# mv of a second mLSTM head made ahead of the first block, with scaled copies of x^T moved behind it

## The chip, the cores and the metric

One core of a Trainium2 chip runs the whole program. The metric is device microseconds for one execution. TensorE is called PE here, its weight loads PEld, VectorE DVE, ScalarE ACT, GpSimd POOL; SyncE (SP) and POOL issue most of the DMAs.

## The reference

One encoder layer on x of 512 positions by 2048 features, all in float32. A normalised x goes through one input projection that feeds an mLSTM branch (4 heads, run forwards and backwards), a differential attention branch (8 heads) and two branch gates; then an output projection, a gated feed-forward part and a last norm follow.

```python
h = _rmsnorm(x, norm1_w[l])
proj = h @ w_in[l]
mq, mk, mv, mo, mg, aq, ak, av, gt = jnp.split(proj, IN_OFFSETS, axis=-1)
q = mq.reshape(B, S, M_HEADS, M_DQK)
v = mv.reshape(B, S, M_HEADS, M_DV)
...
h_fwd = _mlstm_scan(q, k, v, ig[0], lf[0])
...
hm = _rmsnorm(hm, mlstm_norm_w[l].reshape(M_HEADS, M_DV))
hm = hm * jax.nn.sigmoid(mo).reshape(B, S, M_HEADS, M_DV)
```

What the change touches is `v`, the values of the four mLSTM heads: 512 positions by 256 columns each, x (normalised) times a 2048 by 256 slice of `w_in`.

## The kernel before, in words

Each float32 product is made of three float32r matmuls: both operands are split into a rounded part (`hi`, a cast on ACT, L149 or L602) and the rest (`lo`, a subtraction on DVE, L150 or L603), and `mm3` (L145) multiplies hi by hi, hi by lo and lo by hi.

The large projections (the block functions `pre_chunk`, `wo_chunk`, `fi_chunk`, `fo_chunk`) use a scheme of seven products instead of eight (`seven`): per group of 512 contraction rows the left side is needed in seven forms, which are quarters of x^T (`X11`, `X12`, `X22`) and sums of quarters (`S1` to `S4`). The first such block makes the attention values (`av0`). The small projections (`aqk`, `mqk`, `mv`, by `proj_a` and `proj_b`) are plain.

Work is written as chunks, generators that yield after some matmuls. `one()` runs the next step of the first chunk in the list; `advance(ns)` runs steps worth so many nanoseconds between the parts of attention and mLSTM; `upto(name)` runs all up to a chunk's end; `until` runs steps until a condition holds. `behind` is a list of small jobs, and `work()` takes one of them at each step. A scheduler then orders the instructions of each engine; each engine runs its own list in order.

At the start `mv_first` (L725) sets up chunk `mv0`: mv of head 0 with the 16 gate columns, 16 steps of 12 matmuls of 128x272. Its left side is x^T itself, one 128x512 tile (`xraw`) per step. The loop over those 16 tiles (L1324 on) loads each, splits it (two 128x256 `hi` on ACT, L602, two `lo` on DVE, L603), and makes two plain float32 scaled copies on ACT (L1337), of which `xfactors` (L1285) makes the sums `S1` to `S4` (on DVE) and splits them. After each group of four tiles the jobs s1, s2, s34 of that group go to `behind`, and after all four groups the eight jobs that make S4 and S3. Then `av0` begins.

The result of mv0 is copied from PSUM by ACT (L732), written to DRAM by POOL (L735), and fetched back when head 0 of the mLSTM begins. Heads 1 to 3 of mv are chunks of 192 matmuls of 128x256 each (`mv_chunk`, L753), which stand among the chunks `mqk` and run as filler between parts of attention and of the mLSTM; their result is scaled and split straight from PSUM (`mv_split`, L744). `mlstm(h)` (L1195) fetches four tiles of the output gate (`mo`) and two rows of running maxima (`nM`) through POOL, makes the weights (`md`, `mw`), the score matmuls (`ms`), splits them (`mah`, `mal`) and multiplies with v (`mn`). `square` (L1358) loads the 16 natural tiles of x (`xnat`) through POOL one after another and squares them on ACT, for the norm.

Buffers that matter: weights `raw` 6, `hi` 3, `lo` 3; 39 tiles of 128x512 (`t_`); 16 tiles of 128x1024 (`x_`); 8 PSUM banks.

Of the kernel before, what the change touches and what calls it, by code (L numbers as in the profile page):

```python
# [12 lines left out]
F32 = mybir.dt.float32  # L13
# [7 lines left out]
P = 128  # L21
# [10 lines left out]
MH = 4  # L32
# [82 lines left out]
def build(ctx, tc, a, out):  # L115
# [21 lines left out]
    def sm(name, n, tag=None, bufs=None):  # L137
        return small.tile([P, n], F32, tag=tag or name, name=name, bufs=bufs)
# [424 lines left out]
    mv0d = [dpool.tile([P, 512], F32, name=f"mv0_d{i}") for i in range(2)]  # L563

    def rope(p, name, scale, key):
        t = t_(f"{name}_t")
# [155 lines left out]

    def mv_first():  # L725
        def post(view):
            g = sm("g_raw", 64, bufs=1)
            env["g"] = g
            for i in range(2):
                raw = t_(f"mv0_{i}")  # L730
                for t in range(2):
                    A.copy(raw[:, t * 256:(t + 1) * 256], view[2 * i + t][:, :256])  # L732
                    V.tensor_copy(g[:, (2 * i + t) * 16:(2 * i + t + 1) * 16],
                                  view[2 * i + t][:, 256:272])
                G.dma_start(mv0d[i], raw)  # L735

        def lhs(kk, t):
            f_ = xf[kk // 4][f"X{t // 2 + 1}{kk % 2 + 1}"]
            sl = slice(t % 2 * P, t % 2 * P + P)
            return [p_[:, kk % 4 // 2, sl] for p_ in f_]  # L740
        chunk("mv0", [a["w_mv0"][i] for i in range(8)], 2, 272,
              lambda n, it: proj_b(n, it, True, lhs, post, lambda kk: work()))

    def mv_split(h, view):  # L744
        vh = ppool.tile([P, NT, 258], F32R, tag="p", name=f"mvh{h}")
        vl = ppool.tile([P, NT, 258], F32R, tag="p", name=f"mvl{h}")
        V.tensor_copy(vh[:, :, 256:258], ones[:, 0:8].rearrange("p (t c) -> p t c", c=2))
        V.tensor_copy(vl[:, :, 256:258], zero[:, 0:8].rearrange("p (t c) -> p t c", c=2))
        for t in range(NT):
            scaled_split(view[t][:, :256], rstd1[:, t:t + 1], vh[:, t, 0:256], vl[:, t, 0:256])  # L750
        mval[h] = (vh, vl)

    def mv_chunk(h):  # L753
        def lhs(kk, t):
            return [p_[:, t * P:(t + 1) * P] for p_ in xs[kk]]

        def post(view):
            mv_split(h, view)
            while h == MH - 1 and len(has) < AH:
                ha_split()  # L760


        def step(kk):
            if kk % 2 == 0:
                ha_fetch()
            elif kk > 4:
                ha_split()
        chunk(f"mv{h}", [a["w_mv"][(h - 1) * 4 + i] for i in range(4)], 4, 256,
              lambda n, it: proj_b(n, it, False, lhs, post, step if h == MH - 1 else None))
# [499 lines left out]
            hm.append(o)  # L1269


    mv_first()
    n1w = const.tile([P, KD], F32, name="c_n1w")
    nc.sync.dma_start(n1w, a["n1w"])


    xraw, xX = [], []

    def xload(again=False):
        k = len(xraw)  # L1280
# [3 lines left out]

    def xfactors(g):  # L1285

        X, out, nm = xX[g], xf[g], f"x{g}"

        def s1():
            X["S"] = half(f"{nm}_S")  # L1290
            V.tensor_tensor(X["S"], X["X21"], X["X22"], ALU.subtract)
            factor(nm, False, out, "S1", X["S"])

        def s2():
            V.tensor_tensor(X["S"], X["S"], X["X11"], ALU.subtract)
            factor(nm, False, out, "S2", X["S"])

        def s34():
            V.tensor_tensor(X["X21"], X["X11"], X["X21"], ALU.subtract)
            V.tensor_tensor(X["X12"], X["X12"], X["S"], ALU.add)  # L1300
        return ([s1, s2, s34], [lambda: factor(nm, False, out, "S4", X["X12"]),
                                lambda: factor(nm, True, out, "S3", X["X21"])])


# [19 lines left out]
    for k in range(KD):  # L1324
        g, j, s_ = k // 4, k % 2 + 1, k % 4 // 2
        if k % 4 == 0:
            xX.append(fresh(f"x{g}"))
# [156 lines left out]
```

## Time and profile before

| what | us |
|---|---|
| median of 3 runs | 2639.59 (2639.15 to 2642.4) |
| the profiled execution, its own time | 2640.17 |
| its span | 2637.6 |
| TensorE busy | 2592.7 (98%) |
| VectorE busy | 2120.6 (80%) |
| ScalarE busy | 1297.7 (49%) |
| GpSimd busy | 240.0 (9%) |

The span is the time between the first and the last instruction of the profile; the profiled execution took 2.6 us more than its span. Matmuls are pipelined, so that a row's duration is longer than the step from one matmul to the next; the step is read from start times. The same holds, to a smaller extent, for ACT and DVE.

### The profile page before, as it was taken

What the parts mean: (1) busy time and instruction counts of PE and PEld (TensorE: products, weight loads), DVE (VectorE), ACT (ScalarE), POOL (GpSimd) and SP (SyncE); (2) the same over time, 40 slices, a digit from 0 to 9 for tenths busy, and PEclk for the clock granted to TensorE, in tenths of its full rate; (3) what the DMA queues carried; (4) which work ended last, traced back from release to release, by engine and by line L of the source; (5) the groups of instructions that cost most, each with busy time, mean ns of one, the idle gap of its engine ahead of it and who ended that gap; (6) DMA issues with size and microseconds to landing.
All of it is one profiled execution on the core that took longest, in us unless ns stands there. A gap on an engine that the chain in (4) does not pass through costs nothing. (4 is left out here: it accounts for less than half of the span.)

```text
span 2637.6 us, 33224 instructions
## 1 busy us (share of the span) xinstructions
PE 2592.7 (98%) x12184; PEld 2160.2 (82%) x12184; DVE 2120.6 (80%) x2684; ACT 1297.7 (49%) x1824; POOL 240.0 (9%) x440
## 2 busy tenths in 40 slices
PE   8999999999999999999999999999999999999998
PEld 7888888878889998887788888888888878788886
DVE  8877888778875675587898887888888879989985
ACT  8544444545543453344464444444444445556554
POOL 1000000011110123100200000000000001212220
PEclk9999999999999999999999999999999999999999
DMA  7655556744432346446755555555554578777772
GB/s 252 231 189 185 200 192 218 244 125 127 121 115 78 122 141 237 176 153 210 264 184 174 195 178 183 182 196 187 180 197 167 175 279 302 253 274 255 244 247 83
DMA packets 161203, 508.97 MB, mean 193 GB/s; under 512 B 21832, under 2 KB 22120, under 8 KB 161040
## 3 DMA queue, kind: packets, MB, share of 16 engines
q1 hardware_dynamic: 110304, 377.68, 41.5%
q0 software_dynamic: 31536, 95.62, 11.2%
q10 hardware_dynamic: 19200, 33.57, 3.6%
q8 instruction: 95, 1.56, 0.2%
q14 instruction: 68, 0.56, 0.1%
HBM read 445.41 MB, written 50.87 MB: 188 GB/s over the span
## 5 line engine op out<-in xcount | busy, mean ns | idle before, releaser
L145 PE MATMUL aqk_b<-xs,whi_aqk 128*128 128x512 f32 x512 | 161.4, 396 | 0.0
L149 ACT CAST whi_fi_Q<-fi_Q_t 128x1024 fp32r<-128x1024 f32 x88 | 92.5, 1052 | 117.8 <-PE fi_b L145 96.1
L145 PE MATMUL fi_a<-whi_fi_Q,h_X 128*128 128x512 f32 x440 | 147.1, 392 | 0.0
L145 PE MATMUL fi_c<-whi_fi_Q,h_S 128*128 128x512 f32 x440 | 144.6, 390 | 0.0
L145 PE MATMUL fi_b<-whi_fi_Q,h_S 128*128 128x512 f32 x352 | 115.5, 389 | 0.0
L145 PEld LDWEIGHTS aqk_b<-xs,whi_aqk 128*128 128x128 f32 x512 | 94.6, 189 | 18.2
L150 DVE TENSOR_TENSOR wlo_fi_Q<-fi_Q_t,whi_fi_Q 128x1024 fp32r<-128x1024 f32 x88 | 106.3, 1218 | 3.2 <-ACT whi_fi_Q L149 3.1
L362 DVE TENSOR_TENSOR raw_fi_e<-raw_fi_e,raw_fi_f 128x1024 f32<-128x1024 f32 x44 | 53.8, 1224 | 63.8 <-DMA raw_fi_e<-in_w_ffi 63.7
L145 PE MATMUL aqk_b<-xs,wlo_aqk 128*128 128x512 f32 x256 | 100.4, 392 | 0.0
L145 PEld LDWEIGHTS fi_c<-whi_fi_Q,h_S 128*128 128x128 f32 x440 | 82.5, 188 | 17.0
L145 PEld LDWEIGHTS fi_a<-whi_fi_Q,h_X 128*128 128x128 f32 x440 | 82.6, 188 | 16.8
L145 PE MATMUL fi_c<-wlo_fi_Q,h_S 128*128 128x512 f32 x220 | 86.0, 391 | 0.6 <-DVE wlo_fi_Q L150 0.6
L145 PE MATMUL fi_a<-wlo_fi_Q,h_X 128*128 128x512 f32 x220 | 85.7, 389 | 0.7 <-DVE wlo_fi_Q L150 0.7
L990 POOL DMA_DIRECT2D fs_X<-fg_X11d x22 | 11.9, 540 | 795.8 <-DVE wlo_fi_Q L150 737.7
L348 DVE TENSOR_TENSOR raw_fi_b<-raw_fi_b,raw_fi_a 128x1024 f32<-128x1024 f32 x44 | 53.8, 1223 | 35.7 <-DMA raw_fi_b<-in_w_ffi 28.1
L149 ACT CAST whi_fi_Q<-raw_fi_e 128x1024 fp32r<-128x1024 f32 x44 | 46.4, 1055 | 72.6 <-PE fi_b L145 54.3
L149 ACT CAST whi_fi_Q<-raw_fi_b 128x1024 fp32r<-128x1024 f32 x44 | 46.5, 1056 | 72.3 <-PE fi_c L145 52.7
L145 PE MATMUL ba_p<-whi_ba,hahl 128*128 128x512 f32 x256 | 82.0, 390 | 0.0
L145 PE MATMUL bm_p<-whi_bm,hmhl 128*128 128x512 f32 x256 | 80.6, 391 | 0.0
L145 PE MATMUL mqk_b<-xs,whi_mqk 128*128 128x512 f32 x256 | 80.4, 394 | 0.0
L149 ACT CAST whi_fi_Q<-raw_fi_f 128x1024 fp32r<-128x1024 f32 x44 | 46.5, 1056 | 68.3 <-PE fi_c L145 63.7
L145 PEld LDWEIGHTS fi_b<-whi_fi_Q,h_S 128*128 128x128 f32 x352 | 66.1, 188 | 13.7
(830 smaller groups left out, 8425.8 us busy)
## 6 DMA issues: line engine op xcount, KB each, us to landing
raw_fi_a<-in_w_ffi SPq DMA_DIRECT2D x44, 512.0 KB, 4.2
raw_fi_b<-in_w_ffi SPq DMA_DIRECT2D x44, 512.0 KB, 4.2
raw_fi_c<-in_w_ffi SPq DMA_DIRECT2D x44, 512.0 KB, 4.3
raw_fi_d<-in_w_ffi SPq DMA_DIRECT2D x44, 512.0 KB, 4.3
raw_fi_f<-in_w_ffi SPq DMA_DIRECT2D x44, 512.0 KB, 3.9
raw_fi_e<-in_w_ffi SPq DMA_DIRECT2D x44, 512.0 KB, 3.9
raw_aqk<-in_w_aqk SPq DMA_DIRECT2D x32, 512.0 KB, 3.5
raw_fo_a<-in_w_ffo SPq DMA_DIRECT2D x20, 512.0 KB, 4.2
```

The source lines that it names most:

```text
L145: T.matmul(dst, lhs[l], rhs[r], start=first and i == 0, stop=last and i == 2, skip_group_check=skip)
L149: A.copy(hi, src)
L150: V.tensor_tensor(lo, src, hi.bitcast(F32), ALU.subtract)
L348: V.tensor_tensor(raws[r12], raws[r12], raws[r11], ALU.add)
L362: V.tensor_tensor(raws[r12], raws[r12], raws[r22], ALU.add)
L990: G.dma_start(got[n], fgd[g][f_].rearrange("p (k c) -> p k c", k=2))
```

## The change

- A second head of mv, `mv1`, becomes a chunk between `mv0` and the first block. Its left side is the split quarters of x^T that mv0 uses, its weights are four loads of 512 KB, and it has 16 steps at which `work()` takes a job.
- The scaled copies of x^T leave the loop over tiles. They are now two jobs per group in `behind` (eight ACT instructions a group), ahead of s1, s2 and s34 of that group.
- All heads of mv are now kept: copied from PSUM by ACT, written to DRAM by POOL (`mv_keep`), fetched back by POOL (`mv_fetch`) and split from there. Head h+1 is fetched ahead of `mlstm(h)`, after `upto("mv{h+1}")`.

```diff
+    def mv_keep(h, view):
+        for i in range(2):
+            raw = t_(f"mv{h}_{i}")
+            for t in range(2):
+                A.copy(raw[:, t * 256:(t + 1) * 256], view[2 * i + t][:, :256])
+            G.dma_start(mvd[h][i], raw)
...
-        chunk("mv0", [a["w_mv0"][i] for i in range(8)], 2, 272,
-              lambda n, it: proj_b(n, it, True, lhs, post, lambda kk: work()))
+        if h == 0:
+            chunk("mv0", [a["w_mv0"][i] for i in range(8)], 2, 272,
+                  lambda n, it: proj_b(n, it, True, lhs, post, lambda kk: work()))
+        else:
+            chunk(f"mv{h}", [a["w_mv"][(h - 1) * 4 + i] for i in range(4)], 4, 256,
+                  lambda n, it: proj_b(n, it, False, lhs, post, lambda kk: work()))
+    mvraw = {}
+    def mv_fetch(h):
+        mvraw[h] = [t_(f"mv{h}r{i}") for i in range(2)]
+        for i in range(2):
+            G.dma_start(mvraw[h][i], mvd[h][i])
+    def mv_split(h):
+        view = [mvraw[h][t // 2][:, t % 2 * 256:t % 2 * 256 + 256] for t in range(NT)]
...
-            mv_split(h, view)
+            mv_keep(h, view)
...
-    mv_first()
+    for h in range(2):
+        mv_first(h)
...
+        X, out, nm = {}, xf[g], f"x{g}"
+        def scaled(j):
+            for i in (1, 2):
+                X[f"X{i}{j}"] = half(f"{nm}_X{i}{j}")
+            for s_ in range(2):
+                k = 4 * g + 2 * s_ + j - 1
+                for i in (1, 2):
+                    A.activation(X[f"X{i}{j}"][:, s_], xraw[k][:, (i - 1) * 256:i * 256], AF.Copy,
+                                 scale=n1w[:, k:k + 1])
...
-        return ([s1, s2, s34], [lambda: factor(nm, False, out, "S4", X["X12"]),
+        return ([lambda: scaled(1), lambda: scaled(2), s1, s2, s34], [lambda: factor(nm, False, out, "S4", X["X12"]),
...
-        for i in range(2):
-            f_, src = f"X{i + 1}{j}", xraw[k][:, i * 256:i * 256 + 256]
-            A.activation(xX[g][f_][:, s_], src, AF.Copy, scale=n1w[:, k:k + 1])
...
-        if h:
+        if h > 1:
             mv_chunk(h)
...
     for h in range(MH):
-        if h:
-            upto(f"mv{h}")
+        upto(f"mqk{h}")
+        mv_split(h)
         if h == MH - 1:
             hm_split()
+        else:
+            upto(f"mv{h + 1}")
+            mv_fetch(h + 1)
         mlstm(h)
```

How the change moves instructions, at three places. First the queue of SyncE at the start (`raw_mv_50` to `raw_mv_70` are the last weights of mv0, `raw_mv_00` and those after it the weights of mv1, `xraw` tiles of x^T from the seventh on, `raw_av` weights of the first block). Before:

```order
L197 DMA raw_mv_50_278<-in_w_mv 128x544
L197 DMA raw_mv_60_280<-in_w_mv 128x544
L197 DMA raw_mv_70_282<-in_w_mv 128x544
L1283 DMA xraw_314<-in_xT 128x512
L1283 DMA xraw_338<-in_xT 128x512
L1283 DMA xraw_362<-in_xT 128x512
L1283 DMA xraw_390<-in_xT 128x512
L197 DMA raw_av_a_732<-in_w_pre 128x1024
L197 DMA raw_av_b_734<-in_w_pre 128x1024
L1283 DMA xraw_420<-in_xT 128x512
L197 DMA raw_av_c_736<-in_w_pre 128x1024
```

And now:

```order
L197 DMA raw_mv_50_278<-in_w_mv 128x544
L197 DMA raw_mv_60_280<-in_w_mv 128x544
L197 DMA raw_mv_70_282<-in_w_mv 128x544
L197 DMA raw_mv_00_288<-in_w_mv 128x1024
L197 DMA raw_mv_10_294<-in_w_mv 128x1024
L1300 DMA xraw_316<-in_xT 128x512
L197 DMA raw_mv_20_318<-in_w_mv 128x1024
L1300 DMA xraw_340<-in_xT 128x512
L197 DMA raw_mv_30_342<-in_w_mv 128x1024
L1300 DMA xraw_364<-in_xT 128x512
L1300 DMA xraw_386<-in_xT 128x512
```

Two of the four loads of mv1's weights now stand ahead of the seventh tile of x^T (`xraw_316`), one ahead of the eighth and one ahead of the ninth; the block's first weights come after all but three of the tiles.

Second, ACT in the same stretch (L602: the `hi` of a tile of x^T; L1337 before and L1312 now: the scaled copies; `whi_mv`: `hi` of mv0's weights). Before:

```order
L602 ACTIVATE x_X_381<-xraw_266,c_n1w 128x256
L602 ACTIVATE x_X_383<-xraw_266,c_n1w 128x256
L1337 ACTIVATE x_X_377<-xraw_266,c_n1w 128x256
L1337 ACTIVATE x_X_379<-xraw_266,c_n1w 128x256
L602 ACTIVATE x_X_380<-xraw_314,c_n1w 128x256
L602 ACTIVATE x_X_382<-xraw_314,c_n1w 128x256
L1337 ACTIVATE x_X_376<-xraw_314,c_n1w 128x256
L149 CAST x_S2h<-x_S 128x512
L1337 ACTIVATE x_X_378<-xraw_314,c_n1w 128x256
L149 CAST whi_mv_50_449<-raw_mv_50_278 128x544
L602 ACTIVATE x_X_381<-xraw_338,c_n1w 128x256
L602 ACTIVATE x_X_383<-xraw_338,c_n1w 128x256
```

And now:

```order
L602 ACTIVATE x_X_379<-xraw_340,c_n1w 128x256
L602 ACTIVATE x_X_381<-xraw_340,c_n1w 128x256
L1312 ACTIVATE x_X_388<-xraw_242,c_n1w 128x256
L1312 ACTIVATE x_X_389<-xraw_242,c_n1w 128x256
L1312 ACTIVATE x_X_388<-xraw_250,c_n1w 128x256
L1312 ACTIVATE x_X_389<-xraw_250,c_n1w 128x256
L1312 ACTIVATE x_X_416<-xraw_246,c_n1w 128x256
L1312 ACTIVATE x_X_417<-xraw_246,c_n1w 128x256
L1312 ACTIVATE x_X_416<-xraw_254,c_n1w 128x256
L1312 ACTIVATE x_X_417<-xraw_254,c_n1w 128x256
L602 ACTIVATE x_X_485<-xraw_364,c_n1w 128x256
L602 ACTIVATE x_X_487<-xraw_364,c_n1w 128x256
```

The scaled copies stood in pairs behind each tile; now the eight of the first group stand in one piece between the eighth tile and the ninth. On PE, 21 of mv1's 192 matmuls now stand ahead of the last matmul of mv0, spread over its last three steps; the other 171 follow it, and then the block.

Third, POOL where the first head of the mLSTM begins (`mv0r`, `mv1r`: heads of mv fetched back; `ha_d<-hn`: the last head of attention written out; `mo`, `nM`: see above). Before:

```order
L1452 DMA mv0r_7827<-mv_d_124 128x512
L1452 DMA mv0r_7828<-mv_d_125 128x512
L1108 DMA ha_d<-hn_7811 128x512
L1200 DMA mo_0_7885<-mo_d_1888 128x256
L1200 DMA mo_0_7885<-mo_d_1892 128x256
L1200 DMA mo_1_7886<-mo_d_1965 128x256
L1200 DMA mo_1_7886<-mo_d_1969 128x256
L1205 DMA nM_0_7891<-negm_d 128x512
L1205 DMA nM_1_7893<-negm_d 128x512
```

And now:

```order
L730 DMA mv_d_128<-mv_0_7987 128x512
L730 DMA mv_d_129<-mv_1_7991 128x512
L757 DMA mv0r_8037<-mv_d_124 128x512
L757 DMA mv0r_8038<-mv_d_125 128x512
L1124 DMA ha_d<-hn_8021 128x512
L757 DMA mv1r_8077<-mv_d_126 128x512
L757 DMA mv1r_8078<-mv_d_127 128x512
L1216 DMA mo_0_8081<-mo_d_2120 128x256
L1216 DMA mo_0_8081<-mo_d_2124 128x256
L1216 DMA mo_1_8082<-mo_d_2197 128x256
L1216 DMA mo_1_8082<-mo_d_2201 128x256
L1221 DMA nM_0_8087<-negm_d 128x512
```

The two writes of head 2 of mv stand ahead of the fetch of head 0, and the fetch of head 1 stands ahead of `mo` and `nM` of head 0. The same holds for heads 1 and 2, with the fetches of heads 2 and 3.

## Rows read from the trace of the kernel before

**Rows 1.** the page: the span, and busy time, share and instructions of each engine
```profile
span 2637.6 us, 33224 instructions
...
PE 2592.7 (98%) x12184; PEld 2160.2 (82%) x12184; DVE 2120.6 (80%) x2684; ACT 1297.7 (49%) x1824; POOL 240.0 (9%) x440
```

**Rows 2.** busy time in three stretches; columns as in the first line
```profile
core 0: us, PE busy (x) PEld busy (x) DVE busy (x) ACT busy (x) POOL busy (x), PEclk, DMA share, GB/s
...
0.00:100.00 100.00, 87.10 (x424) 74.43 (x425) 84.30 (x132) 74.01 (x151) 15.09 (x35) 0.97 0.73 247
...
20.00:40.00 20.00, 16.47 (x105) 14.94 (x106) 20.00 (x40) 19.99 (x48) 0.00 (x0) 0.92 0.68 235
...
800.00:900.00 100.00, 100.00 (x691) 92.81 (x691) 56.21 (x116) 39.81 (x78) 8.24 (x13) 1.00 0.27 93
```

**Rows 3.** longest wait of TensorE in the whole run: total us, times, longest
```profile
PE mv_p L145 <- ACT whi_mv L149: 6.8, 1, 6.8
```

**Rows 4.** timeline of TensorE, 20 to 64 us: start, us, instruction, [idle before]
```profile
20.29 0.28 PE L145 MATMUL mv_p<-whi_mv,x_X 128*128 128x272 f32 x1
...
35.49 0.39 PE L145 MATMUL mv_p<-whi_mv,x_X 128*128 128x272 f32 x1 [1.82 <-DVE x_X L603]
...
43.65 0.40 PE L145 MATMUL av_a<-whi_av_Q,x_X 128*128 128x512 f32 x1
...
46.87 0.39 PE L145 MATMUL av_c<-wlo_av_Q,x_S1h 128*128 128x512 f32 x1
...
51.63 0.39 PE L145 MATMUL av_b<-whi_av_Q,x_S2l 128*128 128x512 f32 x1
...
63.91 0.39 PE L145 MATMUL av_a<-whi_av_Q,x_X 128*128 128x512 f32 x1
```

**Rows 5.** timeline of TensorE inside one later head of mv
```profile
941.08 0.28 PE L145 MATMUL mv_p<-wlo_mv,xs 128*128 128x256 f32 x1
...
944.68 0.28 PE L145 MATMUL mv_p<-wlo_mv,xs 128*128 128x256 f32 x1
```

**Rows 6.** busy time in two stretches of 2 us, columns as in rows 2
```profile
22.00:24.00 2.00, 1.54 (x13) 1.32 (x11) 2.00 (x6) 2.00 (x5) 0.00 (x0) 1.00 1.02 391
...
38.00:40.00 2.00, 2.00 (x11) 2.00 (x11) 2.00 (x6) 1.99 (x5) 0.00 (x0) 0.50 0.01 2
```

**Rows 7.** timelines of VectorE, 41 to 45 us, and of ScalarE, 23 to 25 us
```profile
41.73 0.88 DVE L603 SCALAR_TENSOR_TENSOR x_X<-xraw,c_n1w,x_X 128x256 fp32r<-128x256 f32 x2
...
42.60 0.69 DVE L1291 TENSOR_TENSOR x_S<-x_X,x_X 128x512 f32<-128x512 f32 x1
...
43.20 1.22 DVE L150 TENSOR_TENSOR wlo_av_Q<-raw_av_a,whi_av_Q 128x1024 fp32r<-128x1024 f32 x1
...
44.34 0.69 DVE L150 TENSOR_TENSOR x_S1l<-x_S,x_S1h 128x512 fp32r<-128x512 f32 x1
...
23.10 0.63 ACT L149 CAST whi_mv<-raw_mv 128x544 fp32r<-128x544 f32 x1
...
23.63 0.91 ACT L602 ACTIVATE x_X<-xraw,c_n1w 128x256 fp32r<-128x256 f32 x2
...
24.44 0.90 ACT L1337 ACTIVATE x_X<-xraw,c_n1w 128x256 f32<-128x256 f32 x2
```

**Rows 8.** tile view of xnat, the natural tiles of x: last line
```profile
DMA to landing us min/median/max: 2.7/6.5/7.6
```

**Rows 9.** timelines of GpSimd, VectorE and TensorE around the first and last mLSTM head
```profile
870.76 1.07 POOL L1205 DMA_DIRECT2D nM<-negm_d  x2
...
876.61 0.29 DVE L1213 TENSOR_TENSOR md<-nM,maskf 128x128 f32<-128x128 f32 x1 [4.43 <-DMA nM<-negm_d]
...
888.89 0.69 DVE L150 TENSOR_TENSOR mal<-mw,mah 128x512 fp32r<-128x512 f32 x1 [0.49 <-ACT mah L149]
...
892.37 0.28 PE L145 MATMUL mn<-mvl,mah 128*128 128x258 f32 x1
...
1010.84 0.39 PE L145 MATMUL mn<-mvh,mah 128*128 128x258 f32 x1 [1.48 <-ACT mah L149]
```

More of the change, by code (lines that the diff above doesn't have):

```diff
@@ L562, in build @@
     had = [dpool.tile([P, 512], F32, name=f"ha{h}_d") for h in range(AH)]
-    mv0d = [dpool.tile([P, 512], F32, name=f"mv0_d{i}") for i in range(2)]
+    mvd = [[dpool.tile([P, 512], F32, name=f"mv{h}_d{i}") for i in range(2)] for h in range(MH)]
     def rope(p, name, scale, key):
@@ L721, in mqk_chunk, with mv_first @@
               lambda n, it: proj_a(n, it, xs, KD, post))
-    def mv_first():
-        def post(view):
-            g = sm("g_raw", 64, bufs=1)
-            env["g"] = g
-            for i in range(2):
[L730 to L735, printed above, removed]
+    def mv_keep(h, view):
[4 more added lines that the diff above has]
+            G.dma_start(mvd[h][i], raw)
+    def mv_first(h):
+        def post(view):
+            mv_keep(h, view)
+            if h == 0:
+                g = sm("g_raw", 64, bufs=1)
+                env["g"] = g
+                for t in range(NT):
+                    V.tensor_copy(g[:, t * 16:(t + 1) * 16], view[t][:, 256:272])
         def lhs(kk, t):
@@ L740, in lhs @@
             return [p_[:, kk % 4 // 2, sl] for p_ in f_]
-        chunk("mv0", [a["w_mv0"][i] for i in range(8)], 2, 272,
-              lambda n, it: proj_b(n, it, True, lhs, post, lambda kk: work()))
-    def mv_split(h, view):
+        if h == 0:
+            chunk("mv0", [a["w_mv0"][i] for i in range(8)], 2, 272,
[10 more added lines that the diff above has]
+        view = [mvraw[h][t // 2][:, t % 2 * 256:t % 2 * 256 + 256] for t in range(NT)]
         vh = ppool.tile([P, NT, 258], F32R, tag="p", name=f"mvh{h}")
@@ L757, in post @@
         def post(view):
-            mv_split(h, view)
+            mv_keep(h, view)
             while h == MH - 1 and len(has) < AH:
@@ L1269, in mlstm @@
             hm.append(o)
-    mv_first()
+    for h in range(2):
+        mv_first(h)
     n1w = const.tile([P, KD], F32, name="c_n1w")
     nc.sync.dma_start(n1w, a["n1w"])
-    xraw, xX = [], []
+    xraw = []
     def xload(again=False):
@@ L1285, in xfactors @@
     def xfactors(g):
-        X, out, nm = xX[g], xf[g], f"x{g}"
+        X, out, nm = {}, xf[g], f"x{g}"
[7 more added lines that the diff above has]
+                                 scale=n1w[:, k:k + 1])
         def s1():
@@ L1326, in build @@
         if k % 4 == 0:
-            xX.append(fresh(f"x{g}"))
             for f_ in ("X11", "X12", "X21", "X22"):
@@ L1334, in build @@
             scaled_split(src, n1w[:, k:k + 1], xf[g][f_][0][:, s_], xf[g][f_][1][:, s_])
-        for i in range(2):
-            f_, src = f"X{i + 1}{j}", xraw[k][:, i * 256:i * 256 + 256]
-            A.activation(xX[g][f_][:, s_], src, AF.Copy, scale=n1w[:, k:k + 1])
         xload()
@@ L1449, in build @@
     upto("mqk0")
-    raw = [t_(f"mv0r{i}") for i in range(2)]
-    for i in range(2):
-        G.dma_start(raw[i], mv0d[i])
+    mv_fetch(0)
     advance(4000)
-    mv_split(0, [raw[t // 2][:, t % 2 * 256:t % 2 * 256 + 256] for t in range(NT)])
     hm = []
```

## The prediction

> **What bounds the kernel now.** I read the page first: PE is busy for 2592.7 us of a span of 2637.6 [rows 1], so 44.9 us are open, and a change pays by closing gaps of PE or by handing PE fewer matmuls. This one leaves their number as it is. Then the windows: 800 to 900 us is 100.00 busy, while the first 100 us hold 87.10, so that 12.9 of the 44.9 us lie at the start [rows 2]. The waits of TensorE put 6.8 of them at its first matmul, for the first weights [rows 3]; nothing in the change touches these. What is left is in the stretch of mv0 and the first block's beginning, which I read instruction by instruction.
>
> From 20 to 40 us PE is busy for 16.47 us, while DVE has 20.00 and ACT 19.99 of 20 [rows 2]: the splits and sums of x^T pace the start. The wait of 1.82 us for DVE's `x_X` is one piece of it [rows 4]. At 22 to 24 us the DMA engines are full too, at 391 GB/s [rows 6]. The granted clock shows a second loss: 0.50 at 38 to 40 us [rows 6], the lower of the two levels, after PE had waited. The block begins at 43.65 us, and its 73rd matmul starts at 63.91 [rows 4].
>
> **Part 1: where mv1 leaves.** 192 matmuls of 128x256 leave a stretch that PE fills. Thirty of them go from 941.08 to 944.68 us, 0.12 us each [rows 5]: 192 x 0.12 = **23.0 us** are saved there, as long as PE always has another piece of filler to run.
>
> **Part 2: where mv1 arrives.** Three things decide what comes back.
>
> (a) When mv0 ends. The order moves ACT's scaled copies behind the tiles. Ahead of the last `hi` of x^T, ACT has 14 copies less (0.40 each [rows 7]), two casts of 128x512 less and one of 128x1024 more; by the 0.53 us of the 128x544 cast [rows 7] the casts nearly cancel, so it has some 5.6 us less to do. DVE, ahead of the last `lo`, has six operations of 128x512 less, at 0.60 (42.60 to 43.20), and two of 128x1024 instead of two (1.14, 43.20 to 44.34) [rows 7]: 3.6 us less. Taken alone, that would have the last `lo` at 42.5 - 3.6 = 38.9 us (the last pair starts at 41.73, 0.40 each [rows 7]).
>
> But the new order has a hole. ACT's cast of mv0's sixth 128x544 weights needs the `hi` buffer of the third, one of three, which PE frees at about 20.3 us, as I place it in PE's timeline [rows 4]. Behind that cast stand the seventh and eighth tile (four `hi`) and the eight copies of the first group in one piece: 20.3 + 0.53 + 4 x 0.40 + 8 x 0.40 = 25.6 us, plus the 0.2 that a first operation takes beyond its step, until the ninth tile's first `hi`. I take 25.8. From there DVE still has 16 `lo` (0.40), two of mv0's weights (by 0.60 x 544/512: 0.63), two 1024s (1.14) and twelve 512s (0.60): 6.4 + 1.3 + 2.3 + 7.2 = 17.2 us, and I add 0.6 for the waits between them. The last `lo` then ends at 43.6 us and mv0 at about 44.0, **0.35 later** than the 43.65 of before.
>
> (b) What of mv1 hides. 21 of its 192 matmuls stand among mv0's last three steps, where PE waits for x^T anyway. The other 171 cost 171 x 0.12 = 20.5 us. They need only what mv0 has used, so they run without a gap, to 64.5 us; meanwhile DVE and ACT make the block's sums.
>
> (c) What the block gains. It loses time now: 21 of its matmuls step from 46.87 to 51.63, 0.227 each [rows 4], so 72 would take 16.3 us, and they took 63.91 - 43.65 = 20.26. Behind mv1 its factors are made, so 4.0 us come back.
>
> Together the 73rd matmul of the block starts at 64.5 + 16.3 = 80.8 instead of 63.91: 16.9 us given, 23.0 saved, **6.1 us gained**.
>
> **Part 3: what is taken back.**
> - Clock. PE still waits while DVE finishes, and before, the same pattern was followed by 0.50 [rows 6]. If mv1's start falls into such a stretch, a matmul there takes twice its time. The bounds are 0 (the stretch ends inside mv0) and the 2.0 us of that whole row; I take **0.6**, since mv0's last steps stand in it first.
> - `square`. POOL now writes mv1 when it ends, at about 64.5 us, and most of the 16 loads of `xnat` stand behind that write. One takes 2.7 to 7.6 us to land [rows 8], so rows of the norm can be late for the block's end. Bounds 0 and 2; I take **0.5**, nearer 0 because the block is long.
> - POOL ahead of heads 0 to 2. The fetch of the next head, two issues of 0.53 [rows 9], now stands ahead of `mo` and `nM`. DVE has already waited 4.43 us for `nM` there, and the last `mal` of that chain starts at 888.89 (0.60 us), while PE reaches the matmul behind it at 892.37 [rows 9]: 2.7 us of margin for about 1.1 us of delay. At the last head, which runs beside `ba`, PE did wait 1.48 us for `mah` [rows 9], and with mv one head shorter heads 1 and 2 move to that company as well. Bounds 0 and 3 x 1.48 = 4.4; I take **1.2**, about one such wait, since the margin covers the first head.
> - At nothing: 12 more copies on ACT and as many DMAs issued by POOL, under an ACT busy for 39.81 of 100 us and a DMA share of 0.27 [rows 2]. If that cover failed, a copy of 128x256, at most the 0.40 of rows 7, would hold up PSUM: 4.8 us for all of them.
>
> Sum: -6.1 + 0.6 + 0.5 + 1.2 = **-3.8 us**. The profiled execution took 2640.17 us, 0.6 above the median of 2639.59, so I forecast 2636.4 for such a run and **2635.8** for the median.
>
> **The rivals.**
>
> *The start runs freely.* ACT's hole costs DVE nothing, because DVE has the first group's sums to do meanwhile. Then the 3.6 us of (a) come in full, mv0 ends near 40 and the block's 73rd matmul starts at 77: 9.7 gained, less 1.2: about 2631. For it: DVE and ACT are the stated pace [rows 2]. Against it: the sums need just those copies. I give it 0.28.
>
> *x^T comes late.* The order puts mv1's weights, 4 x 524 KB, ahead of the seventh to ninth tile, and each also waits for a weight buffer that DVE frees. At 391 GB/s [rows 6] 2.1 MB are 5.4 us. If the tiles are that late, mv0 ends near 49, mv1 hides somewhat more, and the gain is gone: 2639 to 2641. Against it: the tiles were loaded well ahead of their use, the DMA share at 38 to 40 us being 0.01 [rows 6]. The same time results if the change doesn't do what it says, because DVE and not PE sets when the block's factors are there: then the block is only put off by mv1's length and nothing is regained. Together 0.26.
>
> One sentence of the Trainium skill bears on this: by "DMA: Bandwidth & Descriptors", section "Issuing engines are not separate DMA queues", transfers started by SP and POOL interleave on the same 16 engines, so that mv1's weights would delay x^T even were they issued elsewhere. The share of 1.02 while x^T and the weights load [rows 6] is in line with it.
>
> *`nM` late, slower than before.* If the fetch ahead of `nM` delays it by more than 2.7 - 1.1 = 1.6 us beyond its own issue, the margin is used up at a time when the made pieces of filler are used up too. PE then stands through the 4.43 us wait [rows 9], and the low clock after it costs about the 1.7 us that half speed takes from 3.4: 6.1 per head. Two of the three heads cost 12.2, in place of the 1.2 I took: 2635.8 + 11 = 2647. For it: POOL's order. Against it: the margin. I give it 0.10.
>
> **How the numbers follow.** My forecast has 0.36, from 2633 to 2638 by the bounds of part 3; the free start 0.28, late x^T or no gain 0.26, late `nM` 0.10. A measurement of this kernel can tell about 0.2%, 5.3 us: faster is below 2634.3, slower above 2644.9. The free start falls below, and of my forecast's own spread about a quarter: 0.28 + 0.08 = 0.36. Slower is 0.10, the rest, 0.54, the same. The range is 2629 (the free start with 2 us less taken back) to 2643 (no gain, with 3 us more of part 3).
>
> **What would show it.** In the profile after: mv0's last matmul near 44 us (40: free start; 49: late x^T, with DVE or ACT waiting for `xraw`); the block's first matmul near 64.5 and its 73rd near 80.8; less PE idle time in the first 100 us, by some 4 to 6; ACT's cast of the sixth weights waiting for PE, and its eight copies in one piece after it. At the first three heads of the mLSTM, DVE's wait for `nM` about 1 us longer, and waits of `mn` for `mah` below 2 us each. The forecast is wrong if PE's idle time at the start stays near 12.9, if PE idles where mv1 left, or if heads 1 and 2 show waits of 4 us and more.

## The result, and the profile after

The changed kernel takes 2653.49 us (median of 5 runs, 2648.92 to 2661.83) where the kernel before takes 2639.59 (median of 5): a ratio of 1.0059, 95% interval 1.0047 to 1.0071. It is slower by some 14 us. I had forecast 2635.8, 3.8 us faster, with a range up to 2643. A second measurement on another chip gave 1.0046 (1.0029 to 1.0063). The profiled execution took 2653.49 us, 13.3 more than that of before.

The page of the changed kernel, the lines that answer to [rows 1]:

```profile
span 2651.2 us, 33252 instructions
...
PE 2593.6 (98%) x12184; PEld 2159.8 (81%) x12184; DVE 2119.9 (80%) x2684; ACT 1303.0 (49%) x1836; POOL 246.0 (9%) x452
```

TensorE's busy time has grown by 0.9 us and its open time from 44.9 to 57.6: the loss is waiting. Windows of the changed kernel, against [rows 2] (columns: start to end, length, busy time of PE, PEld, DVE, ACT and POOL, then PEclk, DMA share, GB/s):

```profile
0.00:100.00 100.00, 82.00 (x509) 74.25 (x510) 73.62 (x127) 71.43 (x152) 16.11 (x37) 0.98 0.68 231
...
20.00:40.00 20.00, 13.89 (x90) 13.03 (x91) 13.25 (x27) 16.97 (x39) 0.00 (x0) 0.91 0.61 213
...
150.00:160.00 10.00, 9.37 (x32) 7.61 (x33) 6.46 (x8) 2.94 (x4) 0.00 (x0) 0.74 0.29 95
...
800.00:900.00 100.00, 99.97 (x608) 88.65 (x608) 59.15 (x110) 38.90 (x73) 7.15 (x10) 1.00 0.24 83
```

The first 100 us hold 82.00 of TensorE where they held 87.10, and DVE, which was full between 20 and 40 us, now has 13.25 of 20. At 800 to 900 us nothing is lost. The timeline of TensorE in the changed kernel, at the points of [rows 4] and further on (start, us, instruction, [idle before <- what ended it]):

```profile
22.24 0.59 PE L145 MATMUL mv_p<-whi_mv,x_X 128*128 128x272 f32 x1 [3.72 <-ACT x_X L602]
...
66.85 0.40 PE L145 MATMUL av_a<-whi_av_Q,x_X 128*128 128x512 f32 x1
...
85.84 0.39 PE L145 MATMUL av_a<-whi_av_Q,x_X 128*128 128x512 f32 x1
...
138.09 0.39 PE L145 MATMUL av_b<-whi_av_Q,x_X 128*128 128x512 f32 x1
...
150.63 0.80 PE L145 MATMUL av_b<-wlo_av_Q,x_X 128*128 128x512 f32 x1 [3.81 <-DVE wlo_av_Q L150]
...
234.60 0.39 PE L145 MATMUL ga_a<-whi_ga_Q,x_X 128*128 128x512 f32 x1
```

These are the first, the 73rd and the 289th of the block's 336 matmuls, its worst wait, and the first matmul of the gate chunk `ga0`, two blocks on. Against before, the block starts 23.2 us later (43.65), its 73rd matmul 21.9 later (63.91), the 289th 25.2 later, and `ga0` 32.0 later. Before, those last two points are

```profile
112.87 0.39 PE L145 MATMUL av_b<-whi_av_Q,x_X 128*128 128x512 f32 x1
...
202.60 0.39 PE L145 MATMUL ga_a<-whi_ga_Q,x_X 128*128 128x512 f32 x1
```

Since mv1 itself is 23.0 us of matmuls, the start has gained nothing, the block has lost 2.0 us up to its 289th matmul, and the stretch from there to `ga0`, where the last matmuls of av mix with the first of mo (I call it the join), has lost 6.8: 96.5 us in place of 89.7. The block's first matmul is the least firm of these landmarks. The kernel with all heads kept (below) has the same order as before on PE, ACT and DVE up to 66 us; in its profiled execution a load of mv0's weights came late (ACT waits 4.86 us for it, TensorE 3.83 up to 13.5 us), and its block starts 2.4 us later than before, but its 73rd matmul at the same time:

```profile
46.08 0.39 PE L145 MATMUL av_a<-whi_av_Q,x_X 128*128 128x512 f32 x1
...
63.85 0.39 PE L145 MATMUL av_a<-whi_av_Q,x_X 128*128 128x512 f32 x1
```

Against that kernel the start of the changed one is 20.8 us later and the block up to its 289th matmul (112.81 there) has lost 4.5; the 25 us of both together stand.

`gm0` starts at 389.3 us, 33.7 later than before, and `bm0` at 1074.8, 11.6 later: the 23.0 us come back there almost whole (22.1). The end adds 1.7.

**The join.** VectorE in the changed kernel, then in the kernel before, at the same instructions:

```profile
142.12 1.23 DVE L356 TENSOR_TENSOR mo_Q_t<-raw_mo_b,raw_mo_c 128x1024 f32<-128x1024 f32 x1
148.21 1.23 DVE L348 TENSOR_TENSOR raw_mo_b<-raw_mo_b,raw_mo_a 128x1024 f32<-128x1024 f32 x1 [4.87 <-DMA raw_mo_b<-in_w_pre]
149.36 2.35 DVE L150 TENSOR_TENSOR wlo_av_Q<-av_Q_t,whi_av_Q 128x1024 fp32r<-128x1024 f32 x2
151.63 1.22 DVE L150 TENSOR_TENSOR wlo_mo_Q<-raw_mo_a,whi_mo_Q 128x1024 fp32r<-128x1024 f32 x1
```

```profile
116.34 1.22 DVE L356 TENSOR_TENSOR mo_Q_t<-raw_mo_b,raw_mo_c 128x1024 f32<-128x1024 f32 x1
...
119.08 2.35 DVE L150 TENSOR_TENSOR wlo_av_Q<-av_Q_t,whi_av_Q 128x1024 fp32r<-128x1024 f32 x2
121.35 1.22 DVE L150 TENSOR_TENSOR wlo_mo_Q<-raw_mo_a,whi_mo_Q 128x1024 fp32r<-128x1024 f32 x1
122.48 1.22 DVE L348 TENSOR_TENSOR raw_mo_b<-raw_mo_b,raw_mo_a 128x1024 f32<-128x1024 f32 x1
```

The sum of mo's weights (L348) has overtaken the last two low parts of av (`wlo_av_Q ... x2`). The load it needs is as late in both kernels (4.8 us from issue to landing now, 4.5 before): SyncE issues it when the sum on L356 has freed its buffer,

```profile
143.37 0.33 SPq L197 DMA_DIRECT2D raw_mo_b<-in_w_pre  x1
```

in the changed kernel, and at 117.58 us before; in both the sum starts 4.8 to 4.9 us later. Before, VectorE made three low parts in that time. Now it stands for 4.87 us with those that TensorE waits for (3.81 us) behind the sum in its queue; and between 150 and 160 us the granted clock is 0.74, part of it at the lower level: up to (1 - 0.74) x 10 = 2.6 us more. No line of the change touches this place; the scheduler's order there has changed with everything ahead of it.

**The start.** ScalarE in the changed kernel:

```profile
18.60 0.64 ACT L149 CAST whi_mv<-raw_mv 128x544 fp32r<-128x544 f32 x1 [1.38 <-issue]
21.68 0.91 ACT L602 ACTIVATE x_X<-xraw,c_n1w 128x256 fp32r<-128x256 f32 x2 [2.43 <-DMA xraw<-in_xT]
...
23.83 0.91 ACT L602 ACTIVATE x_X<-xraw,c_n1w 128x256 fp32r<-128x256 f32 x2 [1.24 <-DMA xraw<-in_xT]
24.65 3.29 ACT L1312 ACTIVATE x_X<-xraw,c_n1w 128x256 f32<-128x256 f32 x8
```

The seventh and the eighth tile of x^T, now queued behind mv1's weights, are late by 2.43 and 1.24 us; TensorE waits 3.72 and goes to the lower clock for a while (0.83 between 20 and 30 us). Behind them stand the eight copies, and the ninth tile's first `hi` comes at 27.84 us. mv0's last matmul comes at 46.22 us, the block at 66.85.

**The block.** GpSimd in the changed kernel:

```profile
67.68 0.54 POOL L730 DMA_DIRECT2D mv_d<-mv  x1 [3.99 <-ACT mv L729]
...
69.38 4.76 POOL L1383 DMA_DIRECT2D xnat<-in_x  x9
```

Nine of the 16 loads of `xnat` come in one run at 69 to 74 us, behind the writes of mv1. Before, the first five came in one run at 47 to 49 us and the others, mostly singly, up to 75 us. TensorE's waits for `wlo_av_Q` follow at 79 (0.57), 83 (1.43) and 96 us (1.50). At the mLSTM, which my rival feared, `mn` waits less than before [rows 9], and so does DVE for `nM` at the first head (1.57 us, 4.43 before):

```profile
1044.30 0.39 PE L145 MATMUL mn<-mvh,mah 128*128 128x258 f32 x1 [0.66 <-ACT mah L149]
```

### The profile page after: what moved, and what is told of

Its sections match the earlier page's. It is cut to its first block, busy times and chain, and to the rows that moved or that the text cites. A ratio compares the mean times of both kernels' runs of the same rounds, so it can differ in the third digit from the quotient of the medians.

```text
span 2651.2 us, 33252 instructions
## 1 busy us (share of the span) xinstructions
PE 2593.6 (98%) x12184; PEld 2159.8 (81%) x12184; DVE 2119.9 (80%) x2684; ACT 1303.0 (49%) x1836; POOL 246.0 (9%) x452
## 5 line engine op out<-in xcount | busy, mean ns | idle before, releaser
L145 PEld LDWEIGHTS fi_a<-whi_fi_Q,h_X 128*128 128x128 f32 x440 | 82.7, 188 | 16.8
L348 DVE TENSOR_TENSOR raw_fi_b<-raw_fi_b,raw_fi_a 128x1024 f32<-128x1024 f32 x44 | 53.8, 1223 | 38.8 <-DMA raw_fi_b<-in_w_ffi 33.8
L149 ACT CAST whi_fi_Q<-raw_fi_f 128x1024 fp32r<-128x1024 f32 x44 | 46.4, 1056 | 68.7 <-PE fi_c L145 65.8
```

The source lines that it names most:

```text
L145: T.matmul(dst, lhs[l], rhs[r], start=first and i == 0, stop=last and i == 2, skip_group_check=skip)
L149: A.copy(hi, src)
L348: V.tensor_tensor(raws[r12], raws[r12], raws[r11], ALU.add)
```

## The experiments

Each ratio is against the kernel before on the same chip, with its 95% interval. Single runs of one kernel spread over 4 to 17 us, so that single terms are read from the traces, at the landmarks above, and the ratios tell whether the sum agrees.

**One part of the change at a time.** First the changed kernel with the copies back in the loop:

```diff
         for i in range(2):
             scaled_split(src, n1w[:, k:k + 1], xf[g][f_][0][:, s_], xf[g][f_][1][:, s_])
+        for i in range(2):
+            A.activation(xX[g][f_][:, s_], src, AF.Copy, scale=n1w[:, k:k + 1])
...
-        return ([lambda: scaled(1), lambda: scaled(2), s1, s2, s34], ...
+        return ([s1, s2, s34], ...
```

> The changed kernel with the scaled copies back in the loop over tiles (mv1 early, all heads kept in DRAM). Four theories. Queue order (the loss of some 14 us against before comes from where things stand in the queues: tiles of x^T behind mv1's weights, xnat behind mv1's writes, the sum of the next block ahead of the low parts of av on VectorE): all three places remain, so 2649 to 2657 us, and the join of av and mo still shows a wait of about 4 us. Moved copies (the eight copies in one piece make the block's factors late): 2642 or less. Kept heads (the fetches ahead of mLSTM): 2653 as the changed kernel. No cover (a chunk ahead of the block costs its time whatever the order): 2653.

Measured: 2652.8 us, 1.0048 (1.0036 to 1.0060); a wait of 3.26 us at the join. The moved copies are not what made the change slow. Then the same lines the other way round, in the kernel before:

> The kernel before with the scaled copies moved to the list of jobs, and nothing else. Queue order: x^T comes as before, xnat as before, but the third sum of mo stands ahead of the last two low parts of av on VectorE here too, so a wait of 3 to 4 us at the join, with some half clock behind it: 2642 to 2647. Moved copies: 2648 to 2654, the loss of the changed kernel at the start. Kept heads and no cover: 2638 to 2642, as before.

Measured: 2646.39 us, 1.0022 (1.0013 to 1.0031). TensorE at the join of that kernel:

```profile
107.86 0.39 PE L145 MATMUL av_b<-whi_av_Q,x_X 128*128 128x512 f32 x1
...
118.62 0.73 PE L145 MATMUL av_b<-wlo_av_Q,x_X 128*128 128x512 f32 x1 [3.30 <-DVE wlo_av_Q L150]
...
202.66 0.39 PE L145 MATMUL ga_a<-whi_ga_Q,x_X 128*128 128x512 f32 x1
```

The copies alone bring the 289th matmul forward from 112.87 to 107.86 us, and the join takes all of it (94.8 us): `ga0` starts at 202.66, where it started before. Up to there this trace shows no loss against before; where behind `ga0` the 5.9 us of the times arise, no run here shows. Third, in the kernel before, the keeping alone (`mv_keep` and `mv_fetch` for all heads, `mv1` in its old place):

```diff
-            mv_split(h, view)
+            mv_keep(h, view)
...
+        upto(f"mqk{h}")
+        mv_split(h)
...
+            upto(f"mv{h + 1}")
+            mv_fetch(h + 1)
```

> The kernel before with all heads of mv copied, written to DRAM and fetched ahead of the mLSTM as in the change; mv1 in its old place, copies in the loop. Queue order, moved copies and no cover: 2638 to 2642, no change by more than 2 us. Kept heads: 2648 or more, with TensorE waiting at the heads of the mLSTM.

Measured: 2640.35 us, 0.9998 (0.9988 to 1.0009). Two writes, two fetches and four copies for each of three more heads cost nothing that can be seen. Fourth, the changed kernel with x^T ahead of mv1's weights:

```diff
     def load(n):
+        if len(xraw) < KD:
+            n = min(n, 8)
```

> The changed kernel, but the weights of mv1 are asked for only when six more tiles of x^T have been, so that the seventh to ninth tile no longer stand behind them. Queue order: TensorE's wait of 3.7 us at 22 us for a tile goes, and with it most of the half clock at 20 to 30 us; xnat and the join stay as they are: 2647 to 2651. Moved copies and kept heads: 2652 to 2655. No cover: mv0 ends sooner but the block waits as much more, 2651 to 2655.

Measured: 2655.64 us, 1.0059 (1.0046 to 1.0072), the ratio of the change itself. The block starts at 63.23 us, 3.6 sooner than in the changed kernel, but its 289th matmul comes at 136.58, only 1.5 sooner. ScalarE waits for no tile at the start any more, but the wait of TensorE that my theory was to remove is still 2.97 us at 21 us:

```profile
17.52 3.29 ACT L1314 ACTIVATE x_X<-xraw,c_n1w 128x256 f32<-128x256 f32 x8
20.73 0.89 ACT L604 ACTIVATE x_X<-xraw,c_n1w 128x256 fp32r<-128x256 f32 x2
```

Now the eight moved copies stand ahead of the next tile's `hi` (as in the kernel with the copies alone, where TensorE waits 2.55 us there); what went are the two waits behind it, 1.39 and 1.95 us. Of the 3.6 us the block loses 2.1 again; the rival "no cover" foretold that, and my theory did not.

**The join.** One edge in the changed kernel's order on VectorE (it makes one instruction stand behind another in the queue):

```diff
+                if nm == "mo0_Q52":
+                    tc.add_manual_dep(ins.ins, pin[0].ins.name, ...NoSync...)
```

where `ins` is the third sum on L348 and `pin[0]` the low part of mo's first weights.

> The changed kernel with one edge on VectorE: the third sum of mo's weights stands behind the low part of mo's first weights, as in the kernel before, and no longer ahead of the last two low parts of av. Join theory (that order costs TensorE the wait of 3.8 us at 150 us and the half clock behind it, 2.6): 2645 to 2649 us, no wait over 1 us at the join. Rival, the waits only move (av and mo are short of weights there, whatever order VectorE has): 2651 to 2655, with a wait of 3 us or more within the next 20 us.

Measured: 2646.73 us, 1.0015 (1.0006 to 1.0023). VectorE in this kernel:

```profile
147.55 2.36 DVE L150 TENSOR_TENSOR wlo_av_Q<-av_Q_t,whi_av_Q 128x1024 fp32r<-128x1024 f32 x2 [0.40 <-ACT whi_av_Q L149]
149.88 1.23 DVE L150 TENSOR_TENSOR wlo_mo_Q<-raw_mo_a,whi_mo_Q 128x1024 fp32r<-128x1024 f32 x1
152.16 1.23 DVE L351 TENSOR_TENSOR raw_mo_b<-raw_mo_b,raw_mo_a 128x1024 f32<-128x1024 f32 x1 [1.05 <-DMA raw_mo_b<-in_w_pre]
```

The sum still waits for its load, 1.05 us, but TensorE does not: its only wait there is 0.42 us, the clock is 1.00 throughout 150 to 160 us, and the join lasts 89.7 us, against 96.5. The same edge in the kernel with the copies alone:

> The kernel before with the scaled copies moved (2646.4 us as run) and the same edge. Join theory: the block began 6.4 us sooner there and lost all of it at the join, so with the edge 2634 to 2640, at or below before. Rival, the waits move: 2644 to 2648.

Measured: 2639.85 us, 0.9990 (0.9979 to 1.0000); `ga0` at 198.58 us, 4 us ahead of before. In all 18 runs the join sorts by this order alone. With the sum ahead (five of them, and the changed kernel) it lasts 94.4 to 96.5 us; with the sum behind (before and thirteen runs) 88.2 to 92.0, 89.7 in before. Against the 89.7 us of before, the six with the sum ahead lose 4.7 to 6.8 us.

The changed kernel once more, beside three others on one chip:

> The changed kernel itself, beside the kernel before and the three others on one chip, so that the price of each mend is read within one chip. Every theory: 10 to 16 us above before, 2650 to 2656, a wait of 3 to 4 us at the join of av and mo and half clock behind it.

Measured: 2653.34 us, 1.0046 (1.0029 to 1.0063), join 96.4 us. The block starts at 67.67 us and takes 70.7 us up to its 289th matmul, 0.8 later and 0.6 less than in the first profile of this kernel.

**The block.** mv1's writes later, so that they do not hold up `xnat`:

```diff
-            G.dma_start(mvd[h][i], raw)
+            if h == 1:
+                later(14000, lambda i=i, raw=raw: G.dma_start(mvd[h][i], raw))
+            else:
+                G.dma_start(mvd[h][i], raw)
```

> The changed kernel with the two writes of mv1 put later in the list of jobs, so that six more loads of xnat stand ahead of them on GpSimd and three to four behind. Theory of the squares (nine loads held up by the writes come in one burst at 69 us, beside the block's weights, and their squares stand ahead of casts of av on ScalarE): the waits of TensorE between 75 and 100 us, 3.5 us, fall to 1 or less, 2648 to 2651. Rival (av's weights are late by themselves, the block uses a buffer as soon as it is free): waits as before, 2652 to 2655.

Measured: 2649.89 us, 1.0028 (1.0014 to 1.0043). The number is the one that the theory of the squares gave, its mechanism is not what happened: GpSimd still issues six loads in one run, at 64.1 us, since they wait for tiles too, and TensorE still waits 2.09 us at 81 us. The edit did not take away what it was meant to. All three mends together (x^T first, writes late, the edge):

> The changed kernel with the tiles of x^T ahead of mv1's weights, mv1's writes later and the edge at the join. If the loss is made of the three orders: 2638 to 2644, the block beginning at 63 us and mo's second group near 153. If mv1 ahead of the block has no cover, whatever the order: 2649 to 2655.

Measured: 2644.4 us, 1.0005 (0.9996 to 1.0013): level with before, not below. The join is whole (89.3 us), the block is not (73.1 us up to its 289th matmul). SyncE and VectorE of this kernel:

```profile
66.36 0.33 SPq L202 DMA_DIRECT2D raw_av_b<-in_w_pre  x1
```

```profile
73.86 1.23 DVE L353 TENSOR_TENSOR raw_av_b<-raw_av_b,raw_av_a 128x1024 f32<-128x1024 f32 x1 [4.77 <-DMA raw_av_b<-in_w_pre]
```

and a window of that kernel:

```profile
66.00:74.00 8.00, 8.00 (x37) 6.64 (x36) 2.83 (x4) 4.20 (x11) 4.65 (x9) 1.00 0.92 243
```

A weight takes 7.5 us from issue to use, while GpSimd issues loads for 4.65 of these 8 us and the DMA engines are at 0.92; the shortest landing of such a weight in this run is 3.4 us. By the Trainium skill ("DMA: Bandwidth & Descriptors", section "Issuing engines are not separate DMA queues") transfers of all issuing engines interleave on the same 16 engines; SyncE's weight behind GpSimd's loads agrees with it. Three tiles used in turn should break the burst:

```diff
-            xnat[n] = t_(f"xnat{n}")
+            if n < 3:
+                ring.append(t_(f"xnat{n}"))
+            xnat[n] = ring[n % 3]
```

With the edge alone, then with x^T first as well, then in the kernel with the copies alone and the edge:

> The changed kernel with the edge at the join (4.6 us above before as run) and xnat in three tiles used in turn, so that its 16 loads can't come in one burst when the block begins. Theory of the burst (the loads of xnat share the DMA engines with the block's weights, raw_av_b takes 7 us to land, VectorE stands in line for it): TensorE's waits between 75 and 100 us fall from 4.5 us to 1.5 or less, and the time to between 2 us below and 2 us above before. Rival (the weights are late because their buffers come free late): waits stay at 4 us, 4 to 6 us above before.

> As the run before it, with the tiles of x^T ahead of mv1's weights too. Theory of the three causes (x^T, burst, join): the block begins near 63.5 us, its waits fall, and the gain forecast at first appears in part: 2 to 5 us below before. Rival (no cover): within 3 us of before, either side, as the run with three mends (2.3 above).

> The kernel before with the scaled copies moved, the edge at the join and the ring of three for xnat, mv1 late as before. Theory of the burst: here seven loads come together at 48 us, and TensorE's wait of 1.35 us at 54 us goes: 3 to 5 us below before. Rival: as without the ring, 1 to 3 us below before.

Measured: 2648.32 us, 1.0020 (1.0011 to 1.0029); 2647.85, 1.0025 (1.0011 to 1.0040); 2651.1, 1.0034 (1.0022 to 1.0047). All three missed. ScalarE with the ring and the edge:

```profile
77.44 0.64 ACT L1394 ACTIVATE xnat<-xnat 128x512 f32<-128x512 f32 x1 [1.57 <-DMA xnat<-in_x]
...
78.07 1.03 ACT L149 CAST whi_av_Q<-raw_av_b 128x1024 fp32r<-128x1024 f32 x1
```

Now the squares wait for their loads on ScalarE, and the casts of av wait behind them: the same fault on another engine. So that the squares' part could be told from the weights' own pace, the next two kernels leave them out (`ssx` is a constant, one `memset` in place of `square`), in the kernel before, and in the changed kernel with x^T first and the edge:

> The kernel before without the 16 loads of xnat and their squares (the sum of squares of each row is a constant, so the norm of x is left out). Theory of the squares: they cost the kernel before little, since its block began while it waited for x^T anyway: 0 to 3 us below before. Rival (weights late by themselves): 0 to 1 below.

> The changed kernel with x^T first and the edge at the join, without the loads and squares of xnat (norm of x left out as in the run before it). Theory of the squares: the waits of TensorE between 64 and 100 us (4 us or more in the runs with them) fall to 1 us, the block's 73rd matmul comes near 80, and the time is 4 to 7 us below that of the kernel before without squares: then mv1 ahead of the block has the cover I forecast. Rival: the waits stay at 3 to 5 us, and the time is within 2 us of the kernel before without squares.

Measured: 2638.35 us, 0.9982 (0.9972 to 0.9991), 4.5 below before, more than either theory gave, and 2636.69, 0.9974 (0.9963 to 0.9985). The block's first and 73rd matmul, without squares in the kernel before:

```profile
45.40 0.40 PE L145 MATMUL av_a<-whi_av_Q,x_X 128*128 128x512 f32 x1
...
62.17 0.39 PE L145 MATMUL av_a<-whi_av_Q,x_X 128*128 128x512 f32 x1
```

and in the changed one with two mends:

```profile
65.79 0.40 PE L145 MATMUL av_a<-whi_av_Q,x_X 128*128 128x512 f32 x1
...
82.13 0.39 PE L145 MATMUL av_a<-whi_av_Q,x_X 128*128 128x512 f32 x1
```

16.8 and 16.3 us, which is the full pace of my sum. The waits at 64 to 100 us are gone, and `raw_av_b`, the weight of the rows above, lands in 3.3 to 4.0 us; with the loads of `xnat`, in the kernel with three mends, it took up to 7.4 (min, median, max, without and with them):

```profile
DMA to landing us min/median/max: 3.3/3.5/4.0
```

```profile
DMA to landing us min/median/max: 3.4/4.3/7.4
```

So the weights are not late by themselves. These two blocks also start later than the ones they are compared with (45.40 after 43.65, 65.79 after 63.23 with x^T first), so that the squares' price is read at the 289th matmul: 111.13 in place of 112.87 us in the kernel before, 1.7 sooner, and with mv1 early

```profile
131.31 0.39 PE L145 MATMUL av_b<-whi_av_Q,x_X 128*128 128x512 f32 x1
```

in place of

```profile
136.58 0.39 PE L145 MATMUL av_b<-whi_av_Q,x_X 128*128 128x512 f32 x1
```

with x^T first, 5.3 sooner. Between the two kernels without squares mv1 ahead of the block puts the first matmul off by 20.4 us in place of 23.0, the 73rd by 20.0, the 289th by 20.2 and `ga0` (200.9 and 219.5 us) by 18.6: it gains 2.6, 3.0, 2.8 and 4.4 us, the last 1.5 of them at the join (89.7 and 88.2 us). By the times the gain is 1.7 us, which my rival gave and not the 4 to 7 of the theory; the ratios differ by 0.0008 and their intervals overlap, so the gain is shown by the traces, not by the times. Last, the squares moved and not left out (`later(30000, ...)` in place of `later(6000, ...)` with x^T first and the edge, 15000 in the kernel with the copies and the edge):

> The changed kernel with x^T first, the edge at the join, and the squares put 24 us of matmul time later in the list of jobs, so that seven stand between the first casts of the block and nine much later. Theory of the squares: waits between 64 and 100 us of 2 us or less, 2 to 5 us below before. Rival: waits of 4 us, 1 to 4 above before.

> The kernel before with the scaled copies moved, the edge at the join (2.3 us below before as run) and the squares 9 us of matmul time later. Theory of the squares: the wait of 1.35 us at 54 us is not theirs, since it comes before most of them; 2 to 4 us below before. Rival: 0 to 2 below, or above where rstd is late.

Measured: 2644.22 us, 1.0002 (0.9993 to 1.0012), still a wait of 1.97 us at 80 us, where nine squares now come much later; and 2639.0, 0.9986 (0.9976 to 0.9997). And the loads issued by SyncE between the weights, one square per 2.6 (2.0) us of matmuls in place of 1.5, the first after 14 (8) us in place of 6:

```diff
-            G.dma_start(xnat[n], a["x"][n // 4]...
+            nc.sync.dma_start(xnat[n], a["x"][n // 4]...
```

> The changed kernel with x^T first, the edge at the join, and the loads of xnat issued by SyncE, each between two weights of the block, one square per 2.6 us of matmul time. Without the squares the block ran at its full pace (73rd matmul 16.3 us after the first) and the kernel was 7 us below before. Theory of the squares (their burst is the harm, not their work): 73rd matmul 16.5 to 18 us after the first, 2 to 6 us below before. Rival (their work on ScalarE and their bytes cost that anyway): 18.5 us or more, within 2 us of before or above.

> The kernel before with the scaled copies moved, the edge at the join and the loads of xnat issued by SyncE among the weights. Theory of the squares: 4 to 7 us below before. Rival: as copies_squares_later, 2 to 4 below, or the weights come late behind an xnat load that waits for a tile, and it is above before.

Measured: 2641.84 us, 0.9995 (0.9982 to 1.0007), and 2641.54, 0.9991 (0.9980 to 1.0002). In the first the 73rd matmul comes 16.4 us after the first, as without squares, with seven squares in that stretch: their work alone is not the harm there. Issuer, spacing and start of the loads changed together, so that these runs don't tell which of them did it. Other squares stand among later pieces (waits of 0.90 us at 90, 1.04 at 111 and 2.48 at 142), and 3.3 us are lost by the 289th. In none of the places tried for the squares did the early block come within 3 us of the 65.5 us that it takes up to its 289th matmul without them.

## Why the prediction was wrong

The sign was wrong. The terms, forecast and as the profiled executions show them:

| term | forecast | measured | from |
|---|---|---|---|
| block's first matmul, against before | +20.9 | +23.2 | 64.5 forecast, 66.85 |
| block up to its 289th matmul | -4.0, +0.5 for `square` | +2.0 | 69.2 us before, 71.2 now |
| the join, to `ga0` | 0 | +6.8 | 89.7, 96.5 |
| `ga0` to `gm0` | 0 | +1.7 | 153.0, 154.7 |
| clock at mv1's start | +0.6 | (in the first row) | |
| mv1 leaves, and the mLSTM | -23.0, +1.2 | -22.1 | 11.6 - 33.7 |
| the rest | 0 | +1.7 | 13.3 - 11.6 |
| sum | -3.8 | +13.3 | |

- **What bounds the kernel** was right for the middle: 800 to 900 us lost nothing when mv1 left (part 1), and the terms at no cost (copies, writes, fetches) cost nothing, as the kernel with all heads kept shows.
- **Part 2 (a), when mv0 ends**: the eight copies did stand in one piece, but the hole did not set the time. ACT's cast waited 1.38 us and came at 18.60 us, not at 20.3; the tiles behind it were late, and the ninth tile's first `hi` came at 27.84 in place of 25.8. I set the end at 44.0; it was 46.2. The missing term was in a rival, that x^T comes late, and its size, 2.3 us, was below what the rival gave. With mv1's weights ahead of the tiles the block starts at 66.9 to 69.7 us (six kernels), with x^T first at 62.4 to 65.8 (six kernels), around my 64.5.
- **Part 2 (c) is the step that failed**, in "Behind mv1 its factors are made, so 4.0 us come back". It failed twice. First, the 4.0 us are the loss of one execution, whose block began early: with the same order, a block that starts 2.4 us later (all heads kept) takes 17.77 us for the 72 matmuls in place of 20.26, so that only 1.5 of the 4.0 us are left to come back. Nor was it factors that TensorE waited for. In the kernel before:

```profile
54.01 0.63 ACT L1364 ACTIVATE xnat<-xnat 128x512 f32<-128x512 f32 x1 [2.77 <-DMA xnat<-in_x]
...
54.64 1.03 ACT L149 CAST whi_av_Q<-raw_av_b 128x1024 fp32r<-128x1024 f32 x1
```

```profile
55.72 0.73 PE L145 MATMUL av_c<-whi_av_Q,x_S1h 128*128 128x512 f32 x2 [0.98 <-ACT whi_av_Q L149]
57.19 0.67 PE L145 MATMUL av_b<-whi_av_Q,x_S2h 128*128 128x512 f32 x1 [0.74 <-ACT whi_av_Q L149]
```

ACT's casts of av's weights stood behind a square that waited for its load, and between 57 and 67 us the granted clock was 0.83 (1.7 us more). Second, mv1 ahead of the block does not take the squares away. Up to the 289th matmul the full pace is 65.3 us (288 x 0.227) and before took 69.2; the seven runs with mv1 early and the squares as they were take 69.7 to 73.4, without squares it is 65.5. In part 3 I gave `square` 0.5 us with a bound of 2, for rows of the norm being late; its loads and its place ahead of casts were not priced. At the 289th matmul it costs 5.3 us with mv1 early and 1.7 before. So the change gains 1.1 us at the block's 73rd matmul (21.9 in place of 23.0) where I had 6.1, and has lost 2.2 by the 289th.
- **The join has no term at all**: I followed the order at the three places that the diff speaks of and took everything from the block's 73rd matmul to mv1's old place as unchanged. One overtaking on VectorE at 142 us cost the join 6.8 us, the largest single miss; with the edge the whole kernel falls from 9 to 14 us above before to 4.6.
- **The rivals**: late `nM`, my case for slower, did not happen; `mn` waited 0.66 us. (By rows 9 the margin there was 2.8 us, not 2.7. The 3.4 us in that rival's price is how long the clock of the kernel before was at 0.50 after the wait at 35 us, from 36.9 to 40.3 us.) "The change doesn't do what it says", the block short of something else than PE, was nearest, but I priced it at no gain.

Of the part that concerns mv1 itself, (a) and (b) hold where x^T comes first, and (c) does not: without squares, with x^T first and the edge, mv1 gains 2.6 us at the block's first matmul (2.15 forecast) and 3.0 at its 73rd (6.1 forecast). That the 4.4 us at `ga0` lie near the 3.8 forecast for the whole is luck, since 1.5 of them come from the join. The loss came from three neighbours: the tiles of x^T, the squares with their loads, and the order at the join. Of the 1.7 us between `ga0` and `gm0` some 1.2 go with mv1's place, since that stretch takes 152.7 to 153.8 us in the eight kernels with mv1 late and 153.5 to 154.8 in the twelve runs with it early; why is open. How much of the last 1.7 us, after `bm0`, belongs to the change is open too: two executions of the changed kernel differ by 3.4 us there. No run with all its work done is below before by more than 0.14%; the lowest, the copies moved with the edge and later squares and mv1 left where it was, is at 0.9986 (0.9976 to 0.9997).

## What to carry to other kernels

When a scheduler sets the order, a change at the start can reorder queues 100 us further on: compare each engine's whole order, and look for an instruction that waits on a DMA and has overtaken one that the bottleneck waits for. Before a lost stretch is called idle time that a change will fill, leave out each suspect of its cause once, and compare when a landmark is reached, not how long a piece took: a piece that starts late loses less to the same wait. Here the loss had another owner than the factors that I had taken for it. A mend that takes a wait off one in-order queue is only one if it does not put the same wait on the next.

## What the runs showed of the hardware

- A wait of TensorE can cost more than its length, and its length alone does not tell when: the six waits of 3.3 to 4.1 us at the join were followed by 10 us at a granted clock of 0.74 to 0.83 (1.7 to 2.6 us more), and in the kernel before so were two of 0.98 and 0.74 us, 1.5 us apart (0.83 between 57 and 67 us); a wait of 2.99 us at 23 us in the kernel with the copies and the edge left it at 1.00.
- A 512 KB weight that lands in 3.4 us at best took over 7 us with the 256 KB loads of another queue beside it, at a DMA share of 0.92, although the two queues are issued by different engines; without those loads the same weight took 3.3 to 4.0 us.
